# Other places for the heads' scores, the heads' values and the gate's sums in a two-layer hybrid trunk

## The chip, the cores and the metric

The kernel runs on one core of one Trainium2 chip. The metric is the device time of one execution in microseconds; lower is better. The kernel before takes 2198.79 us, the median of 3 runs (2198.11 to 2200.05).

## What is computed

Two decoder layers over 256 tokens of width 2048, batch 1, all in float32. Layer 0 mixes tokens with forgetting attention (16 heads of 128), layer 1 with dilated attention (8 heads, three groups of queries and keys of width 128 for each, shared values of width 256). After each mixer comes an MLP of width 8192 with a squared ReLU. Every sub-layer adds into one residual stream and reads it through an RMS norm.

```python
def reference(x, ...):
    for i in range(DEPTH):                      # DEPTH = 2
        h = rms_norm(x, mix_norm_g[i])
        if i % 2 == 0:
            mix = fox_attention(h, ...)
        else:
            mix = dilated_attention(h, ...)
        x = x + mix
        h = rms_norm(x, mlp_norm_g[i])
        x = x + (relu(h @ mlp_w_up[i]) ** 2) @ mlp_w_down[i]
    return x
```

Forgetting attention: queries and keys are normed per head, log_f = log_sigmoid(f + b_f) is summed along the tokens to c, and the causal scores q·k/sqrt(128) + c(query) − c(key) go through a softmax and onto the values. Dilated attention: for each of three patterns (dilation 1, 4, 16, span 128) scores get a linear penalty on the distance and a mask, and the three patterns share one softmax over all their keys, which is then applied to the head's values.

## The kernel before

**Products.** Nearly all work is products of the 256 tokens with weight matrices of 2048 rows, cut into blocks of 512 columns. `product` (line 297) makes one such block: 16 steps over the contraction, 128 rows each. To keep float32's precision, weights and activations are each split into a high and a low part, and three of the four partial products are made; with two blocks of 128 tokens that is six matmuls of 512 columns in a step (lines 308 to 310). The results stand in two of four PSUM banks named `acc`. The weights come by DMA as `raw`; ScalarE casts them to `wh` (line 279), VectorE subtracts to get `wl` (line 280), two steps' worth at a time, five such pairs in flight.

**Jobs between the steps.** Everything else is written as Python generators, which the class `Jobs` runs between the steps of the products. After each step `product` calls `jobs.tick()`, and every job that is due writes its next piece of work. `yield 3` in a job means "go on three steps from now", `yield 0` "go on at once", and `yield` with a key means "go on when that key is done". So the numbers in the yields are places in the written order of the program, counted in steps of whatever product is running. They fix no time: a planner takes the written order as a priority, reserves buffers, adds the waits and makes one queue for each engine. Each engine works its queue in that order, so a matmul of a head that waits holds up the product's matmuls behind it.

**The forgetting layer.** The loop at the end of `trunk` runs over four groups j of four heads. Each group makes three products: queries, keys, values. `qk_chain` (line 404) follows the query product and the key product: it norms, transposes (line 431) and splits into high and low halves (line 446), and marks its key done nine steps after its product's end. In group 0, `gate` (line 516) stands between the first two products, and its chain makes the summed log gates: transposes, a long series of small VectorE operations that ends with `lf` (line 562), then `yield 4`, then six small matmuls into `pc` (lines 565 to 567), the copy `c_q`, and the negated transpose `negc`. The four jobs `fox_head` of a group are started ahead of the value product. Each waits for queries, keys, gate and mask, then `2 * hh` steps, and then writes: the scores into one PSUM bank `sc` (lines 502, 505 and 594, eight matmuls), their eviction into `s_f` and the row maximum on VectorE (lines 600, 603); a step later the exponential on ScalarE; a step later the normalization on VectorE; two steps later three transposes into `ptp` (line 477) and their evictions; when the values are there (`v_chain`, line 450, after the value product), two steps more, and then `pv`: four terms, five matmuls, into another bank `po` of the same pool, evicted by ScalarE and VectorE (lines 471, 472) into `oTf`, which the out projection reads.

**The dilated layer.** `dilated` (line 673) runs over four groups q4 of two heads: three products for queries and keys (one for each pattern), one for the values. The two jobs `dil_head` wait for all three and then `2 * i` steps. Each makes three scores, a step apart, adds the distances on VectorE into one tile `sd` (line 646), takes the maximum over all three (line 652), exponentials on ScalarE (line 655), the sum of the three on VectorE (lines 660, 661) and the normalization into `p_d` (line 663), then transposes, waits for values and two steps, and calls `pv` for two halves of 128 value columns, one directly behind the other.

**Buffers that matter.** The pool `ps_sc` has two banks for scores, for pv's results and for the gate; the pool `ps_tp` has two for transposes. `sd` has one buffer for both heads, `sel` (the gate's selection matrix of a group) one, the score tiles of the forgetting heads four. Queries, keys and values of a group have one buffer each.

The walk through the jobs, from `Jobs._run`:

```python
        for job in list(self.live):
            while job[0] <= self.now and (job[1] is None or job[1] in self.done):
                try:
                    got = next(job[2])
                except StopIteration:
                    self.live.remove(job)
                    break
                if isinstance(got, int):
                    job[0], job[1] = self.now + got, None
                    if not got:
                        continue
                else:
                    job[1] = got
```

Of the kernel before, what the change touches and what calls it, by code (L numbers as in the profile page):

```python
# [17 lines left out]
P = 128  # L18
D = 2048
S = 256  # L20
# [67 lines left out]
def trunk(ctx: ExitStack, tc, x, fox_w_in, fox_b_f, fox_q_gain, fox_k_gain, fox_w_out, dil_w_in,  # L88
# [197 lines left out]
    def in_turn(w, apart=NC // 2):  # L286
        return w.rearrange("p (b h n) -> p b n h", n=apart, h=2)
# [174 lines left out]

    def pv(pt_sb, vt, cols, o_hi, o_lo, name):
        for i, c in enumerate(cols):
            po = ps_sc.tile([P, 512], F32, tag="sc", name=f"po_{name}_{i}")
            whole, v_hi, v_lo = vt
            p_hi, p_lo, p_whole = pt_sb
            for v, p, first in ((v_hi, p_hi, True), (v_hi, p_lo, False), (v_lo, p_hi, False)):
                nc.tensor.matmul(po[:, 0:S], v[:, c:c + P], in_turn(p, P), start=first, stop=False)
            nc.tensor.matmul(po[:, P:S], whole[:, c:c + P], p_whole, start=False, stop=True)  # L470
            nc.scalar.copy(o_hi[i], po[:, 0:S])
            nc.vector.tensor_sub(o_lo[i], po[:, 0:S], o_hi[i].bitcast(F32))
# [26 lines left out]
    def scores(ps, t, q, k, i, stop):  # L499
        (q_whole, q_hi, q_lo), (k_whole, k_hi, k_lo) = q, k  # L500
        if t == 0:
            nc.tensor.matmul(ps[:, 0:P], q_whole[:, i, :], k_whole[:, i, :], start=True, stop=stop)
            return
        for x, (a, b) in enumerate(((q_hi, k_hi), (q_hi, k_lo), (q_lo, k_hi))):
            nc.tensor.matmul(ps[:, P:3 * P], a[:, i, :], in_turn(b[:, i, :], P // 2), start=x == 0, stop=stop and x == 2)


    def block(p_tile):
        at = (0, P, 2 * P)
        return lambda b: p_tile[:, at[b]:at[b] + P]  # L510
# [12 lines left out]
    def gate_chain(tag, pf):  # L523
        yield (tag, "rstd")
        tri = work.tile([P, P], F32, tag="s", name="tri", bufs=4)
        nc.gpsimd.memset(tri, 1.0)
        nc.gpsimd.affine_select(out=tri, in_=tri, compare_op=ALU.is_ge, fill=0.0, base=0,
                                pattern=[[1, P]], channel_multiplier=-1)
        ones = work.tile([P, P], F32, tag="s", name="ones", bufs=4)
        nc.gpsimd.memset(ones, 1.0)  # L530
        f = work.tile([2 * FH, S], F32, tag="s", name="g_f", bufs=4)
        nc.vector.tensor_copy(f, pf)
        yield 3
        pft = ps_sc.tile([P, NT, 2 * FH], F32, tag="sc", name="pft")
        for t in range(NT):
            nc.tensor.transpose(pft[:, t, :], f[:, t * P:(t + 1) * P], ident[:2 * FH, :2 * FH])
        z = small.tile([P, NT, FH], F32, tag="g_z", name="g_z", bufs=1)
        for t in range(NT):
            r = rstd[tag][:, t:t + 1]
            nc.vector.scalar_tensor_tensor(z[:, t, :], pft[:, t, 0:FH], r, bf, ALU.mult, ALU.add)  # L540
            nc.vector.scalar_tensor_tensor(z[:, t, :], pft[:, t, FH:2 * FH], r, z[:, t, :], ALU.mult, ALU.add)

        neg = small.tile([P, NT, FH], F32, tag="g_n", name="g_n", bufs=1)
        nc.vector.tensor_scalar(neg, z, -1.0, None, ALU.mult)
        nc.vector.tensor_tensor(neg, neg, z, ALU.min)
        e = small.tile([P, NT, FH], F32, tag="g_e", name="g_e", bufs=1)
        nc.scalar.activation(e, neg, AF.Exp)
        yield 1
        u = small.tile([P, NT, FH], F32, tag="g_u", name="g_u", bufs=1)
        nc.vector.tensor_scalar(u, e, 2.0, None, ALU.add)  # L550
        nc.vector.reciprocal(u, u)
        nc.vector.tensor_mul(u, e, u)
        u2 = small.tile([P, NT, FH], F32, tag="g_u2", name="g_u2", bufs=1)
        nc.vector.tensor_mul(u2, u, u)
        s = small.tile([P, NT, FH], F32, tag="g_s", name="g_s", bufs=1)
        nc.vector.tensor_scalar(s, u2, 1.0 / 19.0, None, ALU.mult)
        for odd in (17, 15, 13, 11, 9, 7, 5, 3):
            nc.vector.scalar_tensor_tensor(s, s, 1.0 / odd, u2, ALU.add, ALU.mult)
        nc.vector.scalar_tensor_tensor(s, s, 1.0, u, ALU.add, ALU.mult)
        nc.vector.tensor_scalar(z, z, 0.0, None, ALU.min)  # L560
        lf = small.tile([P, NT, FH], F32, tag="g_lf", name="g_lf", bufs=1)
        nc.vector.scalar_tensor_tensor(lf, s, -2.0, z, ALU.mult, ALU.add)
        yield 4
        pc = ps_sc.tile([P, NT, FH], F32, tag="sc", name="pc")
        nc.tensor.matmul(pc[:, 0, :], tri, lf[:, 0, :], start=True, stop=True)
        nc.tensor.matmul(pc[:, 1, :], ones, lf[:, 0, :], start=True, stop=False)
        nc.tensor.matmul(pc[:, 1, :], tri, lf[:, 1, :], start=False, stop=True)
        nc.vector.tensor_copy(c_q, pc)
        yield 1
        pct = ps_sc.tile([FH, S], F32, tag="sc", name="pct")  # L570
        for t in range(NT):
            nc.tensor.transpose(pct[:, t * P:(t + 1) * P], c_q[:, t, :], ident)
        ct = work.tile([FH, S], F32, tag="s", name="g_ct", bufs=4)
        nc.vector.tensor_scalar(ct, pct, -1.0, None, ALU.mult)
        zero = work.tile([P, S], F32, tag="s", name="g_zero", bufs=4)
        nc.vector.memset(zero, 0.0)
        nc.vector.tensor_copy(negc, zero)
        nc.vector.tensor_copy(negc[0:FH, :], ct)
        nc.vector.tensor_sub(negc[32:32 + FH, :], ct, negc[0:FH, :].bitcast(F32))
        jobs.done.add("gate")  # L580

    def fox_head(j, hh, qT, kT, vt, sel):
        h = 4 * j + hh
        yield ("fq", j)
        yield ("fk", j)
        yield "gate"
        yield "mask"
        yield 2 * hh
        ps = ps_sc.tile([P, 512], F32, tag="sc", name=f"sc_f{h}")
        for t in range(NT):  # L590
            at = ps[:, t * P:t * P + (t + 1) * P]
            n = (t + 1) * P
            scores(ps, t, qT[hh // 2], kT[hh // 2], hh % 2, False)
            nc.tensor.matmul(at, sel[:, hh, :], negc[:, 0:n], start=False, stop=True)
        s = work.tile([P, 3 * P], F32, tag="s", name=f"s_f{h}", bufs=4)
        nm = small.tile([P, NT], F32, tag="nm", name=f"nm_f{h}")
        den = small.tile([P, NT], F32, tag="den", name=f"den_f{h}")
        spans = [slice(0, P), slice(P, 3 * P)]
        for t in range(NT):
            nc.vector.scalar_tensor_tensor(s[:, spans[t]], ps[:, spans[t]], c_q[:, t, h:h + 1],  # L600
                                           tables["mask"][:, spans[t]], ALU.add, ALU.add)
        for t in range(NT):
            nc.vector.tensor_reduce(nm[:, t:t + 1], s[:, spans[t]], AX.X, ALU.max, negate=True)
        yield 1
        for t in range(NT):
            nc.scalar.activation(s[:, spans[t]], s[:, spans[t]], AF.Exp, bias=nm[:, t:t + 1],
                                 accum_out=den[:, t:t + 1])
        yield 1
        nc.vector.reciprocal(den, den)
        for t in range(NT):  # L610
            nc.vector.tensor_scalar_mul(s[:, spans[t]], s[:, spans[t]], den[:, t:t + 1])
        yield 2
        pt_sb = p_transposed(block(s), f"f{h}")
        yield ("fv", j)
        yield 2
        if ("f", h // 2) not in oT:
            oT["f", h // 2] = tuple(
                act.tile([P, 2, S], F32R, tag=f"aT{x}", name=f"oTf{x}_{h}", bufs=KC // 2) for x in "hl")
        hi, lo = oT["f", h // 2]
        pv(pt_sb, vt, [hh * P], [hi[:, h % 2, :]], [lo[:, h % 2, :]], f"f{h}")  # L620
        jobs.done.add(("of", h))

    def make_sel(j):
# [10 lines left out]
    def dil_head(q4, i, qTs, kTs, vt):  # L634
        h = 2 * q4 + i
        for g in range(3):
            yield ("dqk", q4, g)
        yield 2 * i
        s = work.tile([P, 3, 3 * P], F32, tag="sd", name=f"sd{h}", bufs=1)
        for g in range(3):  # L640
            yield ("table", g)
# [23 lines left out]
        pt_sb = p_transposed(block(p), f"d{h}")  # L665
        yield ("dv", q4)
        yield 2
        hi, lo = (act.tile([P, 2, S], F32R, tag=f"aT{x}", name=f"oTd{x}_{h}", bufs=KC // 2) for x in "hl")
        oT["d", h] = hi, lo
        pv(pt_sb, vt, [i * S, i * S + P], [hi[:, 0, :], hi[:, 1, :]], [lo[:, 0, :], lo[:, 1, :]], f"d{h}")  # L670
        jobs.done.add(("od", h))

    def dilated(tag):
# [112 lines left out]
    for j in range(4):  # L786
# [3 lines left out]
        vt = values(f"fv{j}")  # L790
# [53 lines left out]
```

## Time and profile before

| | before |
|---|---|
| median of 3 runs | 2198.79 us (2198.11 to 2200.05) |
| the profiled execution | 2198.39 us, of it 2196.7 us span of the instructions |
| instructions | 29876 |
| TensorE matmuls busy | 2182.1 us, 99% of the span |
| TensorE weight loads busy | 1938.2 us, 88% |
| VectorE busy | 1373.5 us, 63% |
| ScalarE busy | 1099.4 us, 50% |
| GpSimd busy | 48.2 us, 2% |
| read from HBM | 421.70 MB, 193 GB/s over the span |
| granted TensorE clock | 1.00 of full speed |

How to read it: times are microseconds from the first instruction. PE is TensorE's matmuls, DVE VectorE, ACT ScalarE, POOL GpSimd, SP SyncE, which issues the DMAs. A row of the timeline gives the start, the busy time, the engine, the line, the operation, the tile written and the tiles read, the shapes and how often; in brackets stands the idle time of the engine before it and what ended it. [...] The chain of waits is followed back from the last instruction to whatever released each one.

### The profile page before, as it was taken

The page shows a single profiled execution, that of the slowest core. Times are in us where ns is not written, and L with a number is a line of the kernel's source. Part 1 is how long each engine was busy: PE and PEld are TensorE (multiplying, and loading weights), DVE is VectorE, ACT ScalarE, POOL GpSimd, SP SyncE. Part 2 cuts the span into 40 slices and gives each one's busy share as a digit, 9 for nine tenths or more (in the row PEclk, how much of TensorE's full clock was granted, in tenths as well). Part 3 has the DMA queues.
Part 4 walks back from the last instruction along what each step waited for, and adds up shares of the span by engine and source line. Part 5 has one row for each costly group of instructions (what it writes and reads, how often), then busy time and mean ns, then how long its engine had stood idle before and what let it go on. Part 6 is the DMA issues. An engine that isn't in the chain of part 4 may idle for free.

```text
span 2196.7 us, 29876 instructions
## 1 busy us (share of the span) xinstructions
PE 2182.1 (99%) x11441; PEld 1938.2 (88%) x11441; DVE 1373.5 (63%) x1799; ACT 1099.4 (50%) x1516; POOL 48.2 (2%) x51
## 2 busy tenths in 40 slices
PE   8999999999999999999999999999999999999999
PEld 7888888998998998998888888888988988988988
DVE  6776686665565565565666766765655665665564
ACT  5555555554454454455555555555544544544442
POOL 1011000000000000000000000000000000000000
PEclk9999999999999999999999999999999999999999
DMA  7566545666666666665665565655656656656664
GB/s 233 163 184 179 177 170 196 197 202 203 202 201 203 202 202 204 201 202 194 192 190 182 173 192 172 193 173 192 202 204 203 202 203 204 200 203 202 201 211 143
DMA packets 248688, 425.76 MB, mean 194 GB/s; under 512 B 16793, under 2 KB 66529, under 8 KB 248545
## 3 DMA queue, kind: packets, MB, share of 16 engines
q1 hardware_dynamic: 248544, 423.86, 60.6%
q8 instruction: 89, 1.46, 0.3%
q14 instruction: 55, 0.44, 0.1%
HBM read 421.70 MB, written 2.10 MB: 193 GB/s over the span
## 4 chain that ended last, share of the span: by engine, by line
PE 95%; ACT 2%; DVE 2%; issue 1%; DMA 0%; SPq 0%; DVEq 0%; ACTq 0%
PE acc L310 20%; PE acc L308 20%; PE acc L309 20%; PE up_n3a_acc L329 5%; PE up_n1a_acc L329 5%; PE up_n3a_sc L329 3%; PE up_n1a_tp L329 3%; PE up_n3a_tp L329 3%; PE up_n1a_sc L329 3%; PE up_n1a_acc L333 3%; PE up_n3a_acc L333 3%; PE up_n1a_sc L333 1%; PE up_n3a_tp L333 1%; PE up_n1a_tp L333 1%; PE up_n3a_sc L333 1%; ACT wh L279 1%
## 5 line engine op out<-in xcount | busy, mean ns | idle before, releaser
L280 DVE TENSOR_TENSOR wl<-raw,wh 128x1024 fp32r<-128x1024 f32 x800 | 978.9, 1224 | 715.4 <-ACT wh L279 710.4
L279 ACT CAST wh<-raw 128x1024 fp32r<-128x1024 f32 x800 | 838.9, 1049 | 901.8 <-PE acc L310 546.3
L308 PE MATMUL acc<-wh,hT_n 128*128 128x512 f32 x896 | 346.2, 387 | 0.0
L309 PE MATMUL acc<-wl,hT_n 128*128 128x512 f32 x896 | 340.2, 380 | 0.0
L310 PE MATMUL acc<-wh,hT_n 128*128 128x512 f32 x896 | 339.8, 379 | 0.0
L308 PE MATMUL acc<-wh,aTh_n1a 128*128 128x512 f32 x512 | 194.5, 380 | 0.0
L309 PE MATMUL acc<-wl,aTh_n1a 128*128 128x512 f32 x512 | 194.0, 379 | 0.0
L310 PE MATMUL acc<-wh,aTl_n1a 128*128 128x512 f32 x512 | 194.0, 379 | 0.0
L308 PE MATMUL acc<-wh,aTh_n3a 128*128 128x512 f32 x512 | 194.0, 379 | 0.0
L309 PE MATMUL acc<-wl,aTh_n3a 128*128 128x512 f32 x512 | 194.0, 379 | 0.0
L310 PE MATMUL acc<-wh,aTl_n3a 128*128 128x512 f32 x512 | 194.0, 379 | 0.0
L310 PEld LDWEIGHTS acc<-wh,hT_n 128*128 128x128 f32 x896 | 169.4, 189 | 23.6
L308 PEld LDWEIGHTS acc<-wh,hT_n 128*128 128x128 f32 x896 | 169.6, 189 | 21.9 <-ACT wh L279 0.4
L309 PEld LDWEIGHTS acc<-wl,hT_n 128*128 128x128 f32 x896 | 169.6, 189 | 21.6 <-DVE wl L280 0.8
L329 PE MATMUL up_n3a_acc<-hT_n,wh 128*128 128x512 f32 x512 | 181.6, 382 | 0.0
L329 PE MATMUL up_n1a_acc<-hT_n,wh 128*128 128x512 f32 x512 | 181.6, 382 | 0.0
L333 PE MATMUL up_n3a_acc<-hT_n,wl 128*128 128x256 f32 x512 | 139.6, 273 | 0.0
L333 PE MATMUL up_n1a_acc<-hT_n,wl 128*128 128x256 f32 x512 | 139.6, 273 | 0.0
L309 PEld LDWEIGHTS acc<-wl,aTh_n3a 128*128 128x128 f32 x512 | 96.8, 189 | 13.8
L310 PEld LDWEIGHTS acc<-wh,aTl_n1a 128*128 128x128 f32 x512 | 96.8, 189 | 13.7
L310 PEld LDWEIGHTS acc<-wh,aTl_n3a 128*128 128x128 f32 x512 | 96.8, 189 | 13.7
L308 PEld LDWEIGHTS acc<-wh,aTh_n3a 128*128 128x128 f32 x512 | 96.8, 189 | 13.6
(721 smaller groups left out, 3159.9 us busy)
## 6 DMA issues: line engine op xcount, KB each, us to landing
raw<-in_mlp_w_up_dram SPq DMA_DIRECT2D x256, 512.0 KB, 4.3
raw<-in_mlp_w_down_dram SPq DMA_DIRECT2D x256, 512.0 KB, 3.9
raw<-in_fox_w_in_dram SPq DMA_DIRECT2D x96, 512.0 KB, 3.8
raw<-in_dil_w_in_dram SPq DMA_DIRECT2D x192, 256.0 KB, 3.0
raw<-in_fox_w_out_dram SPq DMA_DIRECT2D x32, 512.0 KB, 3.8
raw<-in_dil_w_in_dram SPq DMA_DIRECT2D x32, 512.0 KB, 3.6
raw<-in_dil_w_out_dram SPq DMA_DIRECT2D x32, 512.0 KB, 3.7
out_dram<-x SPq DMA_DIRECT2D x8, 256.0 KB, 5.5
```

Source lines behind the costliest of these rows:

```text
L279: nc.scalar.copy(hi, raw)
L280: nc.vector.tensor_sub(lo, raw, hi.bitcast(F32))
L308: nc.tensor.matmul(acc[t], ah[:, tok], hi, start=first, stop=False)
L309: nc.tensor.matmul(acc[t], ah[:, tok], lo, start=False, stop=False)
L310: issued["product"] = nc.tensor.matmul(acc[t], al[:, tok], hi, start=False, stop=last)
L329: issued["product"] = nc.tensor.matmul(banks[b], hi[:, i, col], in_turn(tokens.rearrange("p x s -> p (x s)"), P // 2), start=first, stop=last)
L333: nc.tensor.matmul(banks[b][:, 0:S], lo[:, i, col], in_turn(tokens[:, 0, :], P // 2), start=False, stop=False)
```

## The change

Four places of jobs are moved. In `gate_chain` the gate's sums stand six steps behind the series on VectorE instead of four. In `fox_head` the scores of head hh stand `2 * hh + 2` steps behind the keys instead of `2 * hh`. In `dil_head` the first scores of head i stand `4 * i + 2` steps behind instead of `2 * i`. `pv` becomes a generator that lets one step pass between its column halves; only the dilated heads have two. What comes later in each job moves with it, as far as the values' arrival doesn't set it. No instruction is added or removed, and none changes its shape.

```diff
@@ -462,6 +462,8 @@
 
     def pv(pt_sb, vt, cols, o_hi, o_lo, name):
         for i, c in enumerate(cols):
+            if i:
+                yield 1
             po = ps_sc.tile([P, 512], F32, tag="sc", name=f"po_{name}_{i}")
@@ -560,7 +562,7 @@
         nc.vector.scalar_tensor_tensor(lf, s, -2.0, z, ALU.mult, ALU.add)
-        yield 4
+        yield 6
         pc = ps_sc.tile([P, NT, FH], F32, tag="sc", name="pc")
@@ -585,7 +587,7 @@
         yield ("fk", j)
         yield "gate"
         yield "mask"
-        yield 2 * hh
+        yield 2 * hh + 2
         ps = ps_sc.tile([P, 512], F32, tag="sc", name=f"sc_f{h}")
@@ -617,7 +619,7 @@
-        pv(pt_sb, vt, [hh * P], [hi[:, h % 2, :]], [lo[:, h % 2, :]], f"f{h}")
+        yield from pv(pt_sb, vt, [hh * P], [hi[:, h % 2, :]], [lo[:, h % 2, :]], f"f{h}")
         jobs.done.add(("of", h))
@@ -635,7 +637,7 @@
         for g in range(3):
             yield ("dqk", q4, g)
-        yield 2 * i
+        yield 4 * i + 2
         s = work.tile([P, 3, 3 * P], F32, tag="sd", name=f"sd{h}", bufs=1)
@@ -667,7 +669,7 @@
-        pv(pt_sb, vt, [i * S, i * S + P], [hi[:, 0, :], hi[:, 1, :]], [lo[:, 0, :], lo[:, 1, :]], f"d{h}")
+        yield from pv(pt_sb, vt, [i * S, i * S + P], [hi[:, 0, :], hi[:, 1, :]], [lo[:, 0, :], lo[:, 1, :]], f"d{h}")
         jobs.done.add(("od", h))
```

## The prediction

> **What bounds the kernel now.** I read the page first, then who waited on TensorE, then TensorE's timeline where the heads' work stands between the products' steps.
>
> ```profile
> span 2196.7 us, 29876 instructions
> ...
> PE 95%; ACT 2%; DVE 2%; issue 1%; DMA 0%; SPq 0%; DVEq 0%; ACTq 0%
> ...
> L280 DVE TENSOR_TENSOR wl<-raw,wh 128x1024 fp32r<-128x1024 f32 x800 | 978.9, 1224 | 715.4 <-ACT wh L279 710.4
> L279 ACT CAST wh<-raw 128x1024 fp32r<-128x1024 f32 x800 | 838.9, 1049 | 901.8 <-PE acc L310 546.3
> ```
>
> TensorE sets the end: 95% of the chain of waits. The weight split (ACT cast, then DVE subtraction) is no rival bound: ACT is idle 901.8 us before its casts, most of it until TensorE gives a buffer back, so the split runs ahead. A microsecond that TensorE no longer waits should come off the end one for one. The run of this profile took 2198.39 us, 1.7 more than its span and 0.4 below the median of 2198.79.
>
> The waits that the change can touch:
>
> ```profile
> PE sc_d L502 <- DVE sd L646: 1.9, 4, 0.5
> ...
> PE pc L565 <- DVE g_lf L562: 0.9, 1, 0.9
> PE po_f L469 <- DVE oTfl L472: 0.3, 1, 0.3
> ```
>
> This view counts 3.1 us, too few: a matmul's modelled end overlaps its successor's start, which hides the first part of a wait. So I go by distances between starts.
>
> **Gate, line 563 (4 to 6 steps).**
>
> ```profile
> 54.04 0.60 PE L431 MATMUL ptq_('fq', 0)_1_633<-ident,qn_('fq', 0)_1_543 128*128 128x128 f32 x4
> 55.50 0.37 PE L565 MATMUL pc<-g_lf,tri 128*128 128x16 f32 x2 [0.86 <-DVE g_lf L562]
> ...
> 56.16 0.46 PE L308 MATMUL acc<-wh,hT_n 128*128 128x512 f32 x1
> 56.46 0.38 PE L309 MATMUL acc<-wl,hT_n 128*128 128x512 f32 x1
> 56.68 0.38 PE L310 MATMUL acc<-wh,hT_n 128*128 128x512 f32 x1
> ```
>
> An undisturbed product matmul starts 0.22 us after the one before it (56.46 to 56.68; finer, the nine between 152.56 and 154.51 in the next fence take 1.95 us, 0.216 each). A step of a product is six of them (two token blocks, three terms), 1.30 us. A matmul modelled at 0.38 us is thus followed after 0.22, and the 0.16 between is what the wait view hides: the sums lost 0.86 + 0.16 = 1.02 us or a little more. Two steps (2.59 us) after the place they had is 1.5 us after lf was there. So far they share this place with the transposes. The first product matmul after fp32 work is followed after 0.30 us instead of 0.22 (56.16 to 56.46), and standing alone the sums pay this 0.08 themselves. **Gain 1.0 us** (1.02 and a little, less 0.08), bounds 0 and 1.1. Later is only negc, which the first scores need after the next product.
>
> **Forgetting heads' scores (2·hh to 2·hh + 2).** Group j = 1, first and second head:
>
> ```profile
> 150.65 0.38 PE L502 MATMUL sc_f<-fkT_0w,fqT_0w 128*128 128x128 f32 x2
> ...
> 152.56 0.38 PE L308 MATMUL acc<-wh,hT_n 128*128 128x512 f32 x1
> ...
> 154.51 0.38 PE L502 MATMUL sc_f<-fkT_0w,fqT_0w 128*128 128x128 f32 x2
> ...
> 155.29 0.38 PE L308 MATMUL acc<-wh,hT_n 128*128 128x512 f32 x1
> ```
>
> The second head's eight matmuls cost 155.29 − 154.51 = 0.78 us. The first head's stretch of 1.91 us holds three product matmuls (0.65): 1.26. The excess of 0.48 us is a wait for the last key halves and the scores torn in two by it. By 152.56 these matmuls have run, so all keys were there, and the new place is not before 150.65 + 2.59 = 153.24. All four heads move alike; the third and fourth still share their places with the transposes of the first and second. **0.48 us × 4 groups = 1.9 us**, bounds 0 and 1.9.
>
> The values of the heads: the four jobs count steps from the end of the third product of the group. Before, pv stands 19, 19, 19 and 21 steps after the key product; now at 19, 19, 21 and 23. The third pv had to wait for one of two score banks:
>
> ```profile
> 169.88 0.38 PE L309 MATMUL acc<-wl,hT_n 128*128 128x512 f32 x1
> 170.20 0.38 PE L469 MATMUL po_f<-pTh_f,fv1h 128*128 128x256 f32 x1
> ...
> 170.78 0.46 PE L310 MATMUL acc<-wh,hT_n 128*128 128x512 f32 x1
> ...
> 173.02 0.27 PE L469 MATMUL po_f<-pTh_f,fv1h 128*128 128x256 f32 x1
> ...
> 173.49 0.46 PE L308 MATMUL acc<-wh,hT_n 128*128 128x512 f32 x1
> ```
>
> It starts 0.32 instead of 0.216 after the matmul before it and takes 0.58 where an undisturbed one takes 0.47: 0.21, and one transposition now joins a pv, so one 0.08 fewer: 0.29. In the last group the wait is longer:
>
> ```profile
> 312.48 0.38 PE L309 MATMUL acc<-wl,oTfh 128*128 128x512 f32 x1
> 313.18 0.38 PE L469 MATMUL po_f<-pTh_f,fv3h 128*128 128x256 f32 x1 [0.33 <-DVE oTfl L472]
> ```
>
> 0.70 instead of 0.32 adds 0.38. **4 × 0.29 + 0.38 = 1.5 us**, bounds 0 and 1.5. The out projection needs the last head at its 16th step (31 after the key product); it is there at 23, so nothing is late.
>
> **Dilated heads (2·i to 4·i + 2; pv's two column parts a step apart).** Before, head 0 has its three scores at steps 9, 10, 11 after the third product, head 1 at 11, 12, 13; now 11, 12, 13 and 15, 16, 17. Group 0:
>
> ```profile
> 1147.03 0.39 PE L502 MATMUL sc_d<-dkT_2w,dqT_2w 128*128 128x128 f32 x2
> ...
> 1148.14 0.38 PE L308 MATMUL acc<-wh,hT_n 128*128 128x512 f32 x1
> ...
> 1153.24 0.38 PE L308 MATMUL acc<-wh,hT_n 128*128 128x512 f32 x1
> 1154.11 0.46 PE L502 MATMUL sc_d<-dkT_2w,dqT_2w 128*128 128x128 f32 x2 [0.49 <-DVE sd L646]
> ...
> 1154.74 0.38 PE L309 MATMUL acc<-wl,hT_n 128*128 128x512 f32 x1
> ```
>
> Two scores cost 1.11, one 0.56. Head 1's third starts 0.87 after a product matmul, 0.65 too late, and takes 0.63: **0.73 us**. The reason: sd has one buffer and the scores two banks, so head 1's first eviction waits until head 0's sums have read sd, and its third score waits for that bank.
>
> ```profile
> 1148.18 0.54 DVE L646 SCALAR_TENSOR_TENSOR sd<-dist,sc_d 128x384 f32<-128x384 f32 x1
> ...
> 1152.24 0.54 DVE L660 TENSOR_TENSOR p_d<-sd 128x384 f32<-128x384 f32 x1
> ...
> 1153.41 1.02 DVE L646 SCALAR_TENSOR_TENSOR sd<-dist,sc_d 128x384 f32<-128x384 f32 x2
> ...
> 1158.93 0.74 DVE L455 SCALAR_TENSOR_TENSOR dv0l<-acc,rstd_n,dv0h 128x512 fp32r<-128x512 f32 x1
> ```
>
> From the end of head 0's third score (1147.03 + 0.56 = 1147.59) to the freed bank (1153.41 + 0.51 = 1153.92) pass 6.33 us. In the new order head 1's third score stands four steps and two scores behind that end: 4 × 1.30 + 1.11 = 6.31 us. So the wait just about disappears. It stays 0 if DVE keeps its pace, and is up to 0.74 if the values' eviction L455, which comes at step 16 in both orders, gets between. The DVE order above has sd straight behind the sums, so I take 0.15 left of it.
>
> pv of both heads:
>
> ```profile
> 1160.68 0.27 PE L469 MATMUL po_d<-pTh_d,dv0h 128*128 128x256 f32 x1
> ...
> 1162.09 0.46 PE L308 MATMUL acc<-wh,hT_n 128*128 128x512 f32 x1
> ...
> 1164.02 0.46 PE L469 MATMUL po_d<-pTh_d,dv0h 128*128 128x256 f32 x2
> ...
> 1165.73 0.46 PE L308 MATMUL acc<-wh,hT_n 128*128 128x512 f32 x1
> 1166.03 0.38 PE L309 MATMUL acc<-wl,hT_n 128*128 128x512 f32 x1
> ```
>
> Head 0: 1.41 + 0.08 for the change from fp32 = 1.49. Head 1: 2.01 less three product matmuls (0.65) = 1.36. A part by itself costs what a forgetting pv does, 0.47 + 0.08 = 0.55, so two cost 1.11: 0.38 and 0.25 less. The split adds no fp32 change, because each part ended with one already. But head 0's pv now stands only two steps (2.6 us) behind its transposition instead of three, and ACT has casts and exponentials in between; of its 0.38 I leave half. Per group 0.73 − 0.15 + 0.19 + 0.25 = 1.02, **4.1 us in four groups**; all would be 1.36 × 4 = 5.4. Nothing behind is late: the next product's chain starts 32 steps on, and the last head is needed in the out projection at step 30 and done at 25.
>
> **Sum.** 1.0 + 1.9 + 1.5 + 4.1 = 8.5 us off 2198.39, or off the median: **2190.3 us**. With everything gained 9.8: 2189.0. No instruction and no DMA is added.
>
> **Rivals.**
> 1. *Buffers, not places.* Head 1 still waits for sd, because one buffer is handed on only when head 0 is through; pv 0 still waits for ACT. Then 0.73 + 0.38 per group stay (4.4 us) and 5.4 are gained: 2193.4. For it: 6.33 against 6.31 leaves no reserve. Against: the place that head 1's third score has now, 1153.46 without the wait, is 5.87 us behind head 0's, and step 17 lies 0.44 further back, two thirds of the 0.65. [...]
> 2. *The places don't decide.* A planner makes the queues and puts an instruction where it expects its inputs: head 1's third score belongs to step 13, which is 1148.14 plus two steps and a score, 1151.3, and stands behind the matmul of 1153.24. If it shifts instructions again to where TensorE stalls, the stalls move along: 2198.8, perhaps 2 either way.
> 3. *Slower: the values' chain cuts in.* At step 16 it now meets head 0's exponential and sums on the way to sd.
>
> ```profile
> 1156.02 0.69 ACT L454 ACTIVATE dv0h<-acc,rstd_n 128x512 fp32r<-128x512 f32 x1 [2.13 <-PE acc L310]
> 1156.71 1.04 ACT L279 CAST wh<-raw 128x1024 fp32r<-128x1024 f32 x1
> ...
> 1159.44 0.68 ACT L457 ACTIVATE dv0w<-acc,rstd_n 128x512 f32<-128x512 f32 x1
> ```
>
> If all of it is queued ahead (0.69 + 1.04 + 0.68 on ACT, 0.74 + 1.22 on DVE), the bank comes 4.4 us late, 17.5 in four groups, against 9.8 gained: 2206.5. It makes the kernel slower from 2.45 us a group. Against it: before, head 0's sums and sd were through by 1153.92, 2.1 us ahead of the values' chain; now it follows closely, but is written behind head 0's work.
>
> **How the numbers follow.** No change can be told within 0.2%, 4.4 us: 2194.4 to 2203.2. The forecast 0.61; rival 1 0.16; rival 2 0.15; rival 3 0.08. The forecast's own range is 2188.4 to 2192.0 (all gained, less 0.6 between runs; pv 0 and sd half kept). Faster takes the forecast and rival 1: 0.77. Same: 0.15. Slower: 0.08. The range for 8 in 10 reaches past rival 1 to 2196.5, into rival 2, and to 2188.0 below.
>
> **What would show it.** In the profile after, TensorE's waits for g_lf, oTfl and sd are gone or under 0.2 us each; the first forgetting head's eight matmuls stand together in 0.78 us; head 1's third dilated score starts about 0.22 us behind a product matmul; pv's two parts stand apart at 0.47 each; the last product ends some 8.5 us earlier. I am wrong if a wait for sd of 0.5 us or more stays in each group (rival 1), if scores stand in the middle of steps again (rival 2), or if dv0l stands between head 0's sums and sd (rival 3).

## The result and the profile after

| | before | after |
|---|---|---|
| median, runs side by side | 2198.45 us of 8 (2197.89 to 2200.16) | 2192.73 us of 8 (2191.75 to 2193.40) |
| the profiled execution | 2198.39 us, span 2196.7 | 2193.09 us, span 2191.4 |
| granted TensorE clock, whole execution | 1.00 | 0.998 |

The ratio is 0.9971 (0.9961 to 0.9981): faster by 0.29%, with an interval from 0.19% to 0.39%; the prediction took 0.2% as the least that can be told from no change. 2192.73 lies inside the range given (2188.0 to 2196.5), 2.4 us above the forecast of 2190.3. The code behind `pv` stands two lines further down in the changed kernel (sd is written in line 648 instead of 646, pc in 567 instead of 565).

Who waited on TensorE in the kernel after, its span ahead (line waited at, what it waited for, us in all, times, longest):

```profile
core 0 of [0], span 2191.4 us
...
PE ptx_n L365 <- issue: 2.4, 1, 2.4
PE acc L308 <- ACT wh L279: 2.1, 1, 2.1
PE spare L116 <- POOL ident masks.py:199: 1.9, 1, 1.9
PE sc_d L504 <- DVE sd L648: 0.8, 4, 0.2
```

The waits for g_lf and oTfl are gone. The wait for sd stays in all four groups, 0.2 us by this view. The three largest stand in the first 30 us of the kernel. From 60 us on, the row for sd is the only one.

A wait view tells what TensorE waited for, not when the products came earlier. For that I compare where the same matmul of each stage starts. Timeline of the kernel before, TensorE: first matmul of the first key product, of the first value product, of the MLP in layer 0, of the MLP in layer 1, and the last product matmul of the kernel.

```profile
42.81 0.38 PE L308 MATMUL acc<-wh,hT_n 128*128 128x512 f32 x1
...
66.83 0.38 PE L308 MATMUL acc<-wh,hT_n 128*128 128x512 f32 x1
...
395.60 0.38 PE L329 MATMUL up_n1a_sc<-hT_n,wh 128*128 128x512 f32 x1
...
1524.81 0.38 PE L329 MATMUL up_n3a_sc<-hT_n,wh 128*128 128x512 f32 x1
...
2192.36 0.38 PE L310 MATMUL acc<-wh,aTl_n3a 128*128 128x512 f32 x1
```

The same five of the kernel after:

```profile
44.46 0.38 PE L308 MATMUL acc<-wh,hT_n 128*128 128x512 f32 x1
...
67.38 0.38 PE L308 MATMUL acc<-wh,hT_n 128*128 128x512 f32 x1
...
393.07 0.38 PE L329 MATMUL up_n1a_sc<-hT_n,wh 128*128 128x512 f32 x1
...
1519.50 0.38 PE L329 MATMUL up_n3a_sc<-hT_n,wh 128*128 128x512 f32 x1
...
2187.04 0.38 PE L310 MATMUL acc<-wh,aTl_n3a 128*128 128x512 f32 x1
```

The distances between these starts sort the whole difference into stages:

| stage | before | after | difference | predicted |
|---|---|---|---|---|
| start, to the key product | 42.81 | 44.46 | +1.65 | 0 |
| key to value product (gate) | 24.02 | 22.92 | −1.10 | −1.0 |
| value product to MLP 0 (forgetting) | 328.77 | 325.69 | −3.08 | −3.4 |
| MLP 0 to MLP 1 (dilated) | 1129.21 | 1126.43 | −2.78 | −4.1 |
| MLP 1 to the last matmul | 667.55 | 667.54 | −0.01 | 0 |
| sum | | | −5.32 | −8.5 |

The moved places brought 6.96 us. The profiled execution shows 5.3 because its first 43 us, in which no job of the change has yet run, took 1.65 longer. So there are two questions: why the dilated groups gave 0.70 each instead of 1.02, and whether the slow start belongs to the change.

**The dilated group.** TensorE in the kernel after, group 0, head 1's third score; then head 0's pv, then the start of its second part:

```profile
1153.73 0.38 PE L310 MATMUL acc<-wh,hT_n 128*128 128x512 f32 x1
1154.32 0.46 PE L504 MATMUL sc_d<-dkT_2w,dqT_2w 128*128 128x128 f32 x2 [0.21 <-DVE sd L648]
...
1154.95 0.38 PE L308 MATMUL acc<-wh,hT_n 128*128 128x512 f32 x1
...
1159.17 0.27 PE L471 MATMUL po_d<-pTh_d,dv0h 128*128 128x256 f32 x1
...
1160.64 0.48 PE L472 MATMUL po_d<-pTw_d,dv0w 128*128 128x128 f32 x2
1160.88 0.46 PE L310 MATMUL acc<-wh,hT_n 128*128 128x512 f32 x1
1161.18 0.27 PE L471 MATMUL po_d<-pTh_d,dv0h 128*128 128x256 f32 x1
...
1161.65 0.46 PE L308 MATMUL acc<-wh,hT_n 128*128 128x512 f32 x1
```

The third score starts 1154.32 − 1153.73 = 0.59 behind a product matmul, 0.374 more than 0.216, and takes 1154.95 − 1154.32 = 0.63, 0.075 more than the 0.556 of the undisturbed ones: 0.45 us of the 0.73 remain. Head 0's first part lies torn between product matmuls from 1159.17 to 1160.88; of these 1.71 us five product matmuls between its pieces are 1.08, so it takes 0.63 where the second part takes 1161.65 − 1161.18 = 0.47: 0.15 remain. The other 0.05 is the first part of head 1, which takes 0.53 in this group. VectorE shows why the score is late. The kernel after, VectorE, around head 0's sums:

```profile
1152.49 0.56 DVE L663 TENSOR_TENSOR p_d<-p_d,sd 128x384 f32<-128x384 f32 x1
1152.97 0.75 DVE L455 SCALAR_TENSOR_TENSOR dv0l<-acc,rstd_n,dv0h 128x512 fp32r<-128x512 f32 x1
1153.63 0.54 DVE L648 SCALAR_TENSOR_TENSOR sd<-dist,sc_d 128x384 f32<-128x384 f32 x1
```

Before, sd's row followed the sums directly. Now the values' subtraction dv0l is queued between them, and sd starts 1153.63 − 1152.97 = 0.66 us later than it could. That is the sign named for rival 3, but with one instruction of its chain, not with all of it.

ScalarE in the same stretch, for the torn pv:

```profile
1159.37 1.06 ACT L279 CAST wh<-raw 128x1024 fp32r<-128x1024 f32 x1
1160.34 0.25 ACT L485 COPY pTw_d<-ptp_d 128x128 f32<-128x128 f32 x1
```

A weight cast of 1.06 us stands ahead of the copy pTw_d, and the matmuls that read it come last, at 1160.64.

### The profile page after: what moved, and what is told of

The parts are those of the page before. It is cut to its first block, busy times and chain, and to the rows that moved or that the text cites. A ratio compares the mean times of both kernels' runs of the same rounds, so it can differ in the third digit from the quotient of the medians.

```text
span 2191.4 us, 29887 instructions
## 1 busy us (share of the span) xinstructions
PE 2179.7 (99%) x11441; PEld 1939.3 (88%) x11441; DVE 1373.8 (63%) x1799; ACT 1100.3 (50%) x1516; POOL 48.2 (2%) x51
## 3 DMA queue, kind: packets, MB, share of 16 engines
q8 instruction: 89, 1.46, 0.3%
## 4 chain that ended last, share of the span: by engine, by line
PE 98%; DVE 1%; DMA 0%; issue 0%; ACT 0%; SPq 0%; DVEq 0%; ACTq 0%
PE acc L308 21%; PE acc L309 21%; PE acc L310 21%; PE up_n1a_acc L329 5%; PE up_n3a_acc L329 5%; PE up_n1a_sc L329 3%; PE up_n1a_tp L329 3%; PE up_n3a_sc L329 3%; PE up_n3a_tp L329 3%; PE up_n3a_acc L333 3%; PE up_n1a_acc L333 3%; PE up_n3a_sc L333 1%; PE up_n3a_tp L333 1%; PE up_n1a_tp L333 1%; PE up_n1a_sc L333 1%; PE ptx_n L365 1%
```

## Experiments

The theory (A): each moved place takes away its own wait, the places don't influence one another, and the slow start is a chance of each execution. What is left in the dilated groups comes from the order on VectorE and ScalarE. The rivals: (B) the start is a consequence of the change; (C) what is left comes from sd having one buffer, whatever the order. In the diffs a line of "..." stands for code left out.

**The kernel before, again** (before_again, no edit).

> The kernel before, unchanged. The queues of both kernels are the same for the first 40 us, yet the products of the changed one reach the gate 1.6 us later, after two stretches of 3.4 us at half clock. [...] Theory B (the change brings it about): clock 1.00 and 42.8 us to the first key product in every execution.

Measured: 2198.87 us of 10 runs (2197.65 to 2199.89), ratio 0.9999 (0.9990 to 1.0009). In its profile the key product starts at 43.84 us, 1.03 later than in the first profile of the same kernel, and the granted clock falls in the same two places as in the kernel after. Busy time of PE, PEld, DVE, ACT and POOL in stretches of 10 us, then the granted clock, the DMA share and GB/s. The kernel before in its first profile, where the next stretch has 1.00 too:

```profile
10.00:20.00 10.00, 9.53 (x45) 6.97 (x45) 7.71 (x9) 7.00 (x13) 0.00 (x0) 1.00 0.96 296
```

The same kernel in the profile of before_again:

```profile
10.00:20.00 10.00, 9.56 (x45) 8.05 (x45) 6.96 (x9) 6.22 (x12) 0.00 (x0) 0.83 0.97 293
20.00:30.00 10.00, 7.58 (x36) 6.32 (x34) 6.72 (x11) 8.27 (x17) 0.20 (x1) 0.88 0.93 295
```

So the slow start doesn't need the change: the unchanged kernel has it too. Of its ten executions five were granted 1.00 over the whole time and took 2197.65 to 2198.30; the other five 0.998 to 0.999 and took 2199.44 to 2199.89.

**The gate's place alone** (gate_only, on the kernel before).

```diff
-        yield 4
+        yield 6
         pc = ps_sc.tile([P, NT, FH], F32, tag="sc", name="pc")
```

> Only the gate's sums move from 4 to 6 steps. If the parts add up: the distance from the first key product's start to the first value product's start falls by 1.0 to 1.1 us (24.02 before, 22.92 with the whole change) and nothing else moves by more than 0.1. Rival (a freed TensorE only meets the next late split): less than 0.5 us is left when the last product ends.

Measured: 2197.20 us (one execution, clock 1.00), span 2195.5. Key to value product 65.70 − 42.78 = 22.92 instead of 24.02: −1.10, and no other stage moves by more than 0.1. The gate's step of the sum holds.

**The forgetting heads' places alone** (fox_only, on the kernel before).

```diff
-        yield 2 * hh
+        yield 2 * hh + 2
         ps = ps_sc.tile([P, 512], F32, tag="sc", name=f"sc_f{h}")
```

> Only the forgetting heads move. If the parts add up: 0.67 us in each of the groups 0 to 2 and 1.06 in group 3, 3.1 us together between the first value product and the MLP, and no change in the dilated layer. Rival (the gain belongs to the gate or to the order elsewhere): under 2 us.

Measured: 2195.21 us, span 2193.5. Value product to MLP 0: 392.46 − 66.78 = 325.68 instead of 328.77: −3.09, as in the kernel after (−3.08). The gate and the dilated layer stay as they were.

**The dilated heads' places without the split of pv** (dil_places, on the kernel before).

```diff
-        yield 2 * i
+        yield 4 * i + 2
         s = work.tile([P, 3, 3 * P], F32, tag="sd", name=f"sd{h}", bufs=1)
```

> Only the dilated heads' scores move; pv's two parts stay together. Theory (pv's split costs nothing and saves no wait of the scores): head 1's third score waits 0.45 us as in the changed kernel, and each group gains 0.6 to 0.8 us. Rival (the split is what frees pv): the group gains only the 0.28 us of the scores, pv 0 costs 1.4 to 1.5 us as before.

Measured: 2197.13 us, span 2195.4. MLP 0 to MLP 1: 1523.57 − 396.79 = 1126.78 instead of 1129.21: −2.43, or 0.61 a group. Head 1's third score is late exactly as in the kernel after (1158.04, 0.60 behind the product matmul of 1157.44, again with 0.21 put down to sd). So the split is not what holds the score up, and in this order of the places it brings the other 0.09 a group.

**The split of pv alone** (pv_split, on the kernel before).

```diff
         for i, c in enumerate(cols):
+            if i:
+                yield 1
...
-        pv(pt_sb, vt, ...)
+        yield from pv(pt_sb, vt, ...)
```

> The kernel before with pv's two column parts a step apart, nothing else. Theory (the split by itself neither costs nor saves): the dilated groups change by less than 0.1 us each. Rival (the split frees the pv banks): 0.2 to 0.6 us less a group.

Measured: 2200.11 us (one execution, clock 0.999), span 2198.4. Each dilated group takes 0.09 to 0.10 us longer than in the kernel before. The split is worth something only together with the later places, so here theory A's claim that the places don't influence one another fails: 0.61 from the places and −0.09 from the split are not the 0.70 of both. What the split disturbs in the old places was not followed further.

**The changed kernel, again** (after_again, no edit).

> The changed kernel, unchanged. Theory A (the start is chance): some executions show clock 1.00 and about 2191.1 us, those with less about 2192.6; the span from the first key product to the end stays at 2146.5 in the profile, within 0.1 (2142.6 to the start of the last product matmul). Theory B (the change brings the clock down): all executions below 1.00.

Measured: 2192.86 us of 6 runs (2191.03 to 2193.14), ratio 0.9970 (0.9957 to 0.9982). Key product to last matmul 2186.82 − 44.26 = 2142.56 us, against 2142.58 in the first profile: behind the start the kernel repeats to 0.02. One of the six was granted 1.00, and that is the fastest, 2191.03; the others had 0.998 or 0.999 and took 2192.52 to 2193.14. With the eight of the first comparison, 13 of 14 executions of the changed kernel were granted less than 1.00. Of the kernel before, in before_again and in the runs beside it, after_again and all_apart, it is 25 of 41. At that chance 13 or 14 of 14 come about once in a hundred times. So that the changed kernel has the slow start more often is not excluded: what is left of rival B is the frequency, and it stays open. Against it: both kernels have the same instructions in the same order on TensorE in their first 40 us, and all_apart, which has them too and the moved places besides, was granted 1.00 in two executions of five.

**The values' subtraction behind head 1's eviction** (values_behind, on the changed kernel). VectorE is told to issue dv0l (and dv1l, dv2l, dv3l) only behind the newest write into sd; sd still has one buffer. In the trace that write is head 1's second eviction and not its first, so the subtraction stands one eviction further back than the expectation says.

```diff
-        nc.vector.scalar_tensor_tensor(halves(v_lo), ...)
+        with behind(*([issued["sd"]] if key[0] == "dv" else [])):
+            nc.vector.scalar_tensor_tensor(halves(v_lo), ...)
...
-            nc.vector.scalar_tensor_tensor(s[:, g, :], ...)
+            issued["sd"] = nc.vector.scalar_tensor_tensor(s[:, g, :], ...)
```

> The changed kernel, and the values' subtraction of the dilated groups (dv0l) is queued on VectorE behind head 1's first eviction into sd. Theory (the 0.66 us of dv0l in front of sd is the wait): head 1's third score starts 0.22 to 0.3 us behind a product matmul and takes 0.56; each group gains 0.3 to 0.45. Rival (one buffer sd is handed on too late whatever stands between): the wait stays above 0.3.

Measured: 2192.16 us, span 2190.5. TensorE of values_behind, group 1, head 1's third score and head 0's pv:

```profile
1245.80 0.38 PE L310 MATMUL acc<-wh,hT_n 128*128 128x512 f32 x1
1246.02 0.38 PE L505 MATMUL sc_d<-dkT_2w,dqT_2w 128*128 128x128 f32 x2
...
1250.79 0.27 PE L472 MATMUL po_d<-pTh_d,dv1h 128*128 128x256 f32 x1
1251.07 0.38 PE L472 MATMUL po_d<-pTl_d,dv1h 128*128 128x256 f32 x1
...
1251.61 0.46 PE L308 MATMUL acc<-wh,hT_n 128*128 128x512 f32 x1
```

Its VectorE ahead of that pv, with head 1's first two evictions:

```profile
1245.23 0.55 DVE L649 SCALAR_TENSOR_TENSOR sd<-dist,sc_d 128x384 f32<-128x384 f32 x1
...
1247.29 0.54 DVE L649 SCALAR_TENSOR_TENSOR sd<-dist,sc_d 128x384 f32<-128x384 f32 x1
1247.76 0.74 DVE L456 SCALAR_TENSOR_TENSOR dv1l<-acc,rstd_n,dv1h 128x512 fp32r<-128x512 f32 x1
...
1249.47 1.22 DVE L280 TENSOR_TENSOR wl<-raw,wh 128x1024 fp32r<-128x1024 f32 x1
1250.60 0.42 DVE L485 TENSOR_TENSOR pTl_d<-ptp_d,pTh_d 128x256 fp32r<-128x256 f32 x1
```

The score is on time: 0.22 behind the product matmul, with one buffer for sd. Rival C falls, and dv0l is shown to be the cause of the 0.45. But a group gains only 0.19 of the 0.45. Head 0's pv now stands together, but its first part takes 1251.61 − 1250.79 = 0.82 instead of the 0.63 of its torn pieces (0.19 given back): its second matmul starts at 1251.07, when VectorE has just written pTl_d, which stands behind a weight subtraction. That dv1l delays pTl_d is not shown: measured from head 0's transposes it starts no later here than in the kernel after (2.73 us against 2.94). Head 1's transposes are torn in two (0.12 more), while its own pv gets 0.04 shorter. More than half of what was won is paid back a few steps later.

**Head 1 a step later** (second_head_later, on the changed kernel).

```diff
-        yield 4 * i + 2
+        yield 5 * i + 2
```

> The changed kernel, head 1 of the dilated layer one step later still (5 i + 2), with one sd. Theory (a place late enough cures it, without a buffer): no wait for sd, each group gains 0.4 to 0.5 us, a little more if head 0's transposes then share a place with head 1's third score. Rival (buffers, not places: the wait moves along): over 0.3 us of it stays.

Measured: 2192.95 us, span 2191.2; a group gets 0.03 us longer, where 0.4 to 0.5 less was expected. The wait for sd is gone and head 0's pv is whole, but everything of head 1 moves, and its transposes are the next in line. TensorE of second_head_later, group 1:

```profile
1255.94 0.38 PE L310 MATMUL acc<-wh,hT_n 128*128 128x512 f32 x1
1256.40 0.70 PE L479 MATMUL ptp_d<-ident,p_d 128*128 128x128 f32 x3
1256.85 0.46 PE L308 MATMUL acc<-wh,hT_n 128*128 128x512 f32 x1
```

They start 0.46 behind a product matmul (0.24 late) and take 0.45 where undisturbed ones take 0.25: 0.45 is lost, as much as the score's wait had cost. They wait for the normalization of p_d, which VectorE writes just then:

```profile
1256.05 0.55 DVE L665 TENSOR_SCALAR p_d<-p_d,den_d 128x128 f32<-128x128 f32 x2
```

Besides, head 0's transposes now share a place with head 1's third score, and the two take 0.23 more there than apart, which uses up what pv gained.

**pv a step later** (dil_pv_later, on the changed kernel).

```diff
-        yield 2
+        yield 3
         hi, lo = (act.tile([P, 2, S], F32R, tag=f"aT{x}", name=f"oTd{x}_{h}", bufs=KC // 2) for x in "hl")
```

> The changed kernel, the dilated heads' pv three steps behind their transposes instead of two. Theory (what is left at pv is ScalarE's and VectorE's backlog behind the transposes): pv 0 stands together and costs 0.47 us a part, each group gains 0.15 to 0.2. Rival (pv costs that anyway): under 0.05.

Measured: 2192.08 us, span 2190.4. Head 0's first part and both parts of head 1 take 0.47 (1252.49 to 1252.96 in group 1, head 0, first part). Head 0's second part now shares its place with head 1's transposes, and the two together cost as much as they did apart. That is 0.20 less a group; the late score stays. This confirms the 0.15 and 0.05 read off the profile after.

**All three together** (all_apart, on the changed kernel): values_behind, dil_pv_later, and head 1's transposes a step later.

```diff
+        with behind(*([issued["sd"]] if key[0] == "dv" else [])):
...
-        yield 2
+        yield 2 + i
...
-        yield 2
+        yield 3
```

> The changed kernel with dv0l queued behind sd, the dilated pv three steps behind, and head 1's transposes one step later. Theory (each wait left in the dilated groups belongs to one place, and curing all of them leaves only the fp32 changes): 0.45 + 0.2 = 0.65 us a group less than the changed kernel, 2.6 in all, extra TensorE time of a group's heads 6.23 us. Rival (VectorE and ScalarE are so full there that a wait cured comes back at the next place): under 0.4 a group.

Measured: 2190.14 us of 5 runs (2188.76 to 2190.32), ratio to the kernel before 0.9955 (0.9942 to 0.9969). Each dilated group is 0.65 us shorter than in the kernel after, 2.60 in four, and 4 × (0.70 + 0.65) = 5.4 shorter than in the kernel before: the whole of what the prediction had as possible (1.36 × 4). TensorE's waits in all_apart from 30 to 2190 us, the whole answer:

```profile
core 0 of [0], span 2188.4 us
engine line waited for: us in total, times, longest us
```

The list is empty: behind the start nothing that this view can see holds TensorE up any more, with one buffer for sd.

**The same, and TensorE kept busy in the start** (all_apart_awake). `wake(n)` writes n transposes of the identity into a spare bank, which nobody reads. Twelve more stand ahead of the first product, and twenty behind its first block of steps, where TensorE otherwise idles (2.46 us in all_apart).

```diff
-        wake(12)
+        wake(24)
...
         yield wait
+        if wait == 8:
+            with behind(issued["product"]):
+                wake(20)
```

> The same with 12 more idle transposes before the first product and 20 more while TensorE waits for x at 24 us. Theory (the half clock of some executions comes from TensorE standing idle in the first 30 us): clock 1.00 in all executions, the first key product at 42.8 to 43.0 us in the profile, a median 1.0 to 1.5 us below the other's and a smaller spread. Rival (the transposes only delay the first product, the clock falls by chance): clock still below 1.00 in half of them, median not lower.

Measured: 2188.89 us of 5 runs (2188.89 to 2188.97), ratio 0.9952 (0.9940 to 0.9965), the fastest of all and 3.8 below the median of the changed kernel. All five were granted 1.00, and the runs lie within 0.08 us of one another. The key product starts at 42.87. Its stretches, as above:

```profile
10.00:20.00 10.00, 8.17 (x42) 6.31 (x40) 7.43 (x9) 6.69 (x12) 0.00 (x0) 1.00 0.94 291
20.00:30.00 10.00, 9.53 (x59) 8.56 (x60) 6.14 (x10) 7.87 (x17) 0.20 (x1) 1.00 0.85 269
```

A second buffer for sd was not tried.

## Why the prediction held, and where it was off

The sign, the mechanism and the range were right; the forecast was 2.4 us low. In the two profiled executions 5.3 of the 8.5 came; the missing 3.2 are 1.3 in the dilated term, 0.3 in the forgetting term and 1.65 in the start, less 0.1 that the gate gave beyond its term.

- **Gate, 1.0.** Measured 1.10, alone and together with the rest. Adding a hidden part to the 0.86 of the wait view was right, but it is 0.24 and not 0.16: in gate_only a product matmul follows these transposes 54.37 − 54.01 = 0.36 behind their start, where the sums came 55.50 − 54.04 = 1.46 behind it, 1.10 later. The 0.08 subtracted for standing alone did not show in the total, because the sums themselves got as much shorter (57.62 − 57.04 = 0.58 us up to the next product matmul, instead of 56.16 − 55.50 = 0.66).
- **Forgetting heads, 1.9 + 1.5 = 3.4.** Measured 3.08. The first head's eight matmuls stand together, as claimed. TensorE of the kernel after, group 1, first head's scores, then the third pv with the transposes that now follow it:

```profile
153.12 0.39 PE L504 MATMUL sc_f<-fkT_0w,fqT_0w 128*128 128x128 f32 x2
...
153.91 0.38 PE L308 MATMUL acc<-wh,hT_n 128*128 128x512 f32 x1
...
171.34 0.27 PE L471 MATMUL po_f<-pTh_f,fv1h 128*128 128x256 f32 x1
...
172.14 0.46 PE L308 MATMUL acc<-wh,hT_n 128*128 128x512 f32 x1
```

  153.91 − 153.12 = 0.79, the 0.78 of an undisturbed head. From 171.34 to 172.14 are 0.80 where the working had 0.47 + 0.25 = 0.72, so the saving of 0.08 for "one transposition now joins a pv" did not come: 4 × 0.08 = 0.3. The pairing of a pv part and transposes in dil_pv_later takes 0.80 as well. The extra 0.38 of the last group did come: groups 0 to 2 gained 0.67 to 0.68 each, the last 1.06.
- **Dilated heads, 1.02 a group.** This is the term that was mis-sized: measured 0.70. Of its parts, the two pv left 0.20, with 0.19 assumed. The score left 0.45 instead of 0.15, and 4 × 0.30 = 1.2 of the 1.3 us are that. The step that failed is "The DVE order above has sd straight behind the sums, so I take 0.15 left of it". It took VectorE's order from the old places, though the same paragraph had said that the values' L455 comes at step 16 in both orders and would cost up to 0.74 if it got between. The place named was right, the value taken within the bounds was not; in values_behind the whole 0.45 goes when this one instruction is moved.
- **Rival 1, buffers.** It asked for a wait for sd of 0.5 us or more. What stayed was 0.45 by starts (0.2 by the wait view), but not because there is one buffer. Four equal gaps were there; values_behind and all_apart remove them with one buffer by another order on VectorE.
- **Rival 2, the planner moves the places back.** The scores of the first forgetting head stand where they were written and the stalls did not follow. Only head 0's pv was still torn.
- **Rival 3, the values' chain.** Its sign appeared in every group, at 0.45 us and not at 4.4: of the chain only the subtraction was queued ahead, and the casts and the weight subtraction were not.
- **The end 8.5 earlier.** 5.3 earlier in the profile. The prediction took the start for equal in both executions; it differs by 1.65, which the last section follows up. The median of 2192.73 lies 0.7 above the forecast's own range (up to 2192.0) and nearer to rival 1's 2193.4 than to the forecast, but by the slow start and the score's wait, not by rival 1's mechanism. Between executions that were granted 1.00 throughout, the median of the five in before_again and the one in after_again, the difference is 2198.10 − 2191.03 = 7.1, the 6.96 of the stages.

## What to carry to other kernels

When a place is moved by several steps, redraw the order of the engine that feeds it, not only the order of the engine that waits: whatever else is due at the new place may now stand in that queue, and one instruction of 0.66 us there cost 0.45 on TensorE. A wait that is moved one place on can be handed to the next consumer (values_behind kept 0.19 of 0.45 us a group, second_head_later nothing), so move the whole chain or count what is late next. And measure stages by the starts of the same instruction in both traces: it separates one stage that differs between executions of the same kernel (here 1.65 us at the start) from what the change did.

## What the runs showed of the hardware

TensorE's clock in the first 32 us differs from one execution to the next of the same program. The start of the kernel after, first the stretches, with the granted clock as the third number from the end:

```profile
10.00:20.00 10.00, 9.82 (x42) 7.45 (x42) 7.49 (x9) 6.78 (x12) 0.00 (x0) 0.83 0.95 293
20.00:30.00 10.00, 7.41 (x32) 6.10 (x32) 6.33 (x11) 7.76 (x16) 0.20 (x1) 0.85 0.92 266
30.00:40.00 10.00, 10.00 (x48) 8.19 (x47) 7.68 (x18) 6.37 (x13) 0.83 (x1) 0.98 0.82 266
```

Then its TensorE timeline, the first product matmul and the place near which the second stretch begins:

```profile
9.91 0.77 PE L308 MATMUL acc<-wh,hT_n 128*128 128x512 f32 x1 [2.06 <-ACT wh L279]
...
27.28 1.08 PE L365 MATMUL ptx_n<-ident,x 128*128 128x128 f32 x4 [2.43 <-issue]
```

In stretches of 1 us from 10 to 13 and from 28 to 30 the view gives a clock of 0.50. At half clock the shares 0.17, 0.15 and 0.02 of 10 us are 2 × 3.4 = 6.8 us: two stretches of 3.4. The first begins at 9.9, as an idle time of TensorE of 2.06 ends; the second at 27.0, shortly before one of 2.43 ends.

In these profiles only the second costs time. One profile, that of fox_only, has the first alone:

```profile
10.00:20.00 10.00, 9.44 (x41) 7.76 (x42) 7.50 (x9) 6.77 (x12) 0.00 (x0) 0.83 0.92 283
20.00:30.00 10.00, 7.81 (x43) 6.50 (x42) 6.41 (x12) 7.95 (x17) 0.20 (x1) 1.00 0.93 283
```

Its key product starts at 42.78, as early as at full clock (42.81 in before, 42.78 in gate_only). dil_places, pv_split, second_head_later and all_apart have the second stretch alone, and their key product starts at 44.02 to 44.22; with both stretches it starts at 43.84 to 44.46. What the first stretch delays is made up behind it, because TensorE idles again until 27.1 either way (27.11 in before, 27.08 in fox_only); behind that it has no idle time up to the key product. By the executions of before_again the slow start costs about 1.5 us (2198.1 against 2199.6). In the five profiles with two stretches (after, before_again, after_again, values_behind and dil_pv_later, each granted 0.998 over the whole execution) these begin 17.1 us apart, while the first begins between 9.9 and 11.2 us. The idle times ahead of the second stretches are 2.4 to 2.6 us, and before has one of 2.67 at full clock: the length of the idle time alone does not decide it here, and what does lower the clock is not shown. Filling both idle times with transposes that nobody reads gave clock 1.00 in five executions of five and a spread of 0.08 us, where all_apart without them had 1.56. Which of the two fillings does it was not tried apart; by the starts above the second should be the one that saves time.
